# One layer of a hybrid decoder on one core: rings of their own for raw weights and norm scratch, a preloaded first output projection, a paired end of the input projection, and a later use of the mixers' room

## Chip, cores and metric

The kernel runs on one core of one Trainium2 chip. The metric is the device time of one execution in microseconds, median of three runs.

## What is computed

One layer (DEPTH is 1) of a decoder trunk, in fp32, on 2048 prompt tokens and on 8 further sequences of one token each (the samples):

```python
h = rmsnorm(x, norm_mix);  p = h @ w_in                     # 1024 -> 31 column tiles of 128, and 12 columns for b, a
y = concat(gdn(p_a), rwkv7(p_b), hgrn2(p_c))                # three mixers, chunked recurrences over 64 tokens
x = x + y @ w_out
h = rmsnorm(x, norm_ffn);  u = silu(h @ w_gate) * (h @ w_up)  # 2816 = 22 tiles of 128
x = x + u @ w_down
y = rmsnorm(x, norm_final)
```

The final states of the three mixers, for the prompt and for the samples, are outputs too.

## The kernel before, in words

Tokens lie on the free axis: four column blocks q = 0 to 3 of 512, 512, 512 and 520 tokens (the last holds the 8 samples and is worked in two halves of 260). Channels lie on the partitions. Every large product is a sum of eight k steps of three matmuls each (`mm3`, lines 369 to 376): operands are split into a high and a low part (ACT copies the high part, DVE subtracts), and high x high, high x low and low x high are added up in one PSUM bank. A product of 8 k steps is thus 24 matmuls of 512 columns.

**Two programs are woven into one.** `emit` (from line 1499) has a generator `gemm()` that yields one product after another: the input projection of q = 0, 1, 2, 3 (31 tiles each, `proj`), then for each q `out_proj(q)` and `ffn(q)`. The mixers (gdn g, rwkv r, hgrn h; 8 units for each q, named g00 = gdn, q 0, unit 0, and so on, last h31) are generators too, run by `Driver.turn`. After each round of mixer steps `turn` emits products until `made` has reached `due`, which grows by `RATES[q]` matmuls a round. `out_proj(q)` waits until all units of q are done. What is emitted so gets its place on the five queues (PE, DVE, ACT, POOL, SP) from a scheduler that works with times of its own. Each queue is worked in order: an instruction that waits, a DMA on SP too, holds up what stands behind it. Every tile pool is a ring: a tile may be written when the tile that had its place `bufs` requests earlier is no longer read. So a ring ties together whatever shares its tag, in the order of requests.

**Rings that the change touches.** Pool `x2` (8 tiles of 128x520) serves three users. `load_w` (line 312) takes two tiles of it for the raw halves of each weight tile of the input projection of q = 0 (line 324); a raw half is loaded (line 328), split by ACT (329) and DVE (330) into a tile of the ring `hl` (4 halves, so two weight tiles), and stored for the later q (337). `stats_x(q)` (for q over 0 called in the middle of the projection of q - 1, at unit number `AT` = 5) takes twelve through `S`: seven squares, the projection's b and a columns `pba`, and `be`, `ba` of the function `ba`. `out_proj` takes eight for the residual x2 (line 531). For q = 1 to 3 the weights come back split (line 344).

**The end of the mixers.** When all mixer units are done, `D.end()` returns and `K.late = 1` is set. From there weights are loaded into the mixers' scratch tiles instead of `hl` (the ring of lane A with 29 tiles, line 318; loads in line 342), four weight tiles ahead (`stream`, `AHEAD`), `bank` uses the mixers' PSUM banks as well, and the FFN's temporaries take lane P. The stores of the final states (`finals`, line 1429) are emitted there too.

**The turn of the blocks.** xs is a ring of 8 tiles, one per k: xs of the next block (`split_x`) or the mixers' output (`out_proj`, line 512: loaded by DMA in line 515 into the low half of an xs tile, then split in place) can be written when the last product that reads that k is past it.

```python
        while self.made < self.due and self.product():      # Driver.turn
            pass
    D.end()                                                  # emit, the end
    K.late, K.lane = 1, "A"
    K.finals()
    while D.product() is not None:
        pass
```

## Time and profile before

| | |
|---|---|
| median of 3 runs | 3219.25 us (3217.04 to 3220.66) |
| profiled execution: its time / its span | 3220.64 us / 3218.8 us |
| PE busy | 3079.2 us (96%), 24812 matmuls |
| DVE, ACT busy | 2194.7 us (68%), 1176.6 us (37%) |
| mean granted clock of PE | 0.973 |
| DMA | 628 MB, 195 GB/s over the span |

The profile page gives sums over the whole span and forty slices of it. Its views used below are tables of stretches (busy time of each engine, granted clock, DMA share), the waits (which engine waited for whom), the instructions in order of time of one engine or of SP's DMA queue (SPq), the groups of instructions by line, and the DMA issues. A granted clock of 1.00 is 2.4 GHz and 0.50 is 1.2 GHz; a mean between them tells what part of a stretch ran at either.

### The profile page before, as it was taken

What the parts mean: (1) busy time and instruction counts of PE and PEld (TensorE: products, weight loads), DVE (VectorE), ACT (ScalarE), POOL (GpSimd) and SP (SyncE); (2) the same over time, 40 slices, a digit from 0 to 9 for tenths busy, and PEclk for the clock granted to TensorE, in tenths of its full rate; (3) what the DMA queues carried; (4) which work ended last, traced back from release to release, by engine and by line L of the source; (5) the groups of instructions that cost most, each with busy time, mean ns of one, the idle gap of its engine ahead of it and who ended that gap; (6) DMA issues with size and microseconds to landing.
All of it is one profiled execution on the core that took longest, in us unless ns stands there. A gap on an engine that the chain in (4) does not pass through costs nothing.

```text
span 3218.8 us, 62719 instructions
## 1 busy us (share of the span) xinstructions
PE 3079.2 (96%) x24812; PEld 2464.1 (77%) x24812; DVE 2194.7 (68%) x5424; ACT 1176.6 (37%) x2051; POOL 12.1 (0%) x41
## 2 busy tenths in 40 slices
PE   8999999989998999999999999999999899999998
PEld 6667777768987677677766777777777678999998
DVE  6884667587678888886978788778767632443334
ACT  5443233244335444544454434253523220221002
POOL 0000000000000000000000000000000000000000
PEclk9989999999998999999999999999999899999999
DMA  9777666656655666677664455556544365755552
GB/s 316 257 245 250 188 188 212 195 158 190 190 179 171 223 231 202 225 239 255 231 215 140 149 171 155 173 183 197 179 152 166 107 215 188 248 174 184 188 185 91
DMA packets 393699, 628.00 MB, mean 195 GB/s; under 512 B 173181, under 2 KB 177533, under 8 KB 393405
## 3 DMA queue, kind: packets, MB, share of 16 engines
q1 hardware_dynamic: 392316, 622.93, 60.1%
q8 instruction: 195, 3.19, 0.4%
q10 hardware_dynamic: 1088, 1.07, 0.1%
q14 instruction: 100, 0.81, 0.1%
HBM read 456.77 MB, written 167.14 MB: 194 GB/s over the span
## 4 chain that ended last, share of the span: by engine, by line
PE 68%; DVE 14%; DMA 9%; ACT 4%; issue 2%; SPq 2%; DVEq 0%; ACTq 0%
PE psp L374 5%; PE psp L376 5%; PE psp L375 5%; PE pd L374 4%; PE pd L375 4%; PE pd L376 4%; PE pfg L374 4%; PE pfg L376 4%; PE pfu L375 4%; PE pfu L374 4%; PE pfu L376 4%; PE pfg L375 4%; DMA rw_wu<-wu 1%; PE pso L374 1%; PE pso L375 1%
## 5 line engine op out<-in xcount | busy, mean ns | idle before, releaser
L374 PE MATMUL psp<-xs,w_in 128*128 128x512 f32 (+1 forms) x1240 | 445.3, 360 | 20.1 <-ACT xs L406 8.4
L375 PE MATMUL psp<-xs,w_in 128*128 128x512 f32 (+1 forms) x1240 | 444.7, 359 | 0.8 <-DVE xs L407 0.8
L376 PE MATMUL psp<-xs,w_in 128*128 128x512 f32 (+1 forms) x1240 | 442.6, 358 | 2.0 <-DVE w_in L330 1.8
L374 PEld LDWEIGHTS psp<-xs,w_in 128*128 128x128 f32 x1240 | 236.1, 190 | 60.2 <-ACT xs L406 9.0
L376 PEld LDWEIGHTS psp<-xs,w_in 128*128 128x128 f32 x1240 | 235.5, 190 | 44.4 <-issue 5.5
L375 PEld LDWEIGHTS psp<-xs,w_in 128*128 128x128 f32 x1240 | 236.0, 190 | 37.3 <-issue 2.7
L592 DVE TENSOR_TENSOR x<-pd,x 128x512 f32<-128x512 f32 (+1 forms) x240 | 137.1, 581 | 105.3 <-PE pd L376 104.1
L374 PE MATMUL pfg<-xhs,w_wg 128*128 128x512 f32 x448 | 181.0, 404 | 4.3 <-ACT w_wg L329 3.4
L375 PE MATMUL pfg<-xhs,w_wg 128*128 128x512 f32 x448 | 180.6, 403 | 2.5 <-DVE xhs L550 2.5
L374 PE MATMUL pd<-u,w_wd 128*128 128x512 f32 x432 | 173.5, 409 | 9.1 <-ACT w_wd L329 3.2
L571 ACT ACTIVATE t<-t 128x512 f32<-128x512 f32 (+1 forms) x110 | 60.0, 546 | 333.1 <-DVE t L570 332.8
L376 PE MATMUL pfg<-xhs,w_wg 128*128 128x512 f32 x448 | 180.5, 403 | 0.3 <-DVE w_wg L330 0.3
L374 PE MATMUL pfu<-xhs,w_wu 128*128 128x512 f32 x448 | 180.1, 402 | 0.0
L375 PE MATMUL pfu<-xhs,w_wu 128*128 128x512 f32 x448 | 180.0, 402 | 0.0
L376 PE MATMUL pfu<-xhs,w_wu 128*128 128x512 f32 x448 | 179.6, 401 | 0.0
L375 PE MATMUL pd<-u,w_wd 128*128 128x512 f32 x432 | 173.7, 403 | 1.6 <-DVE u L360 1.6
L376 PE MATMUL pd<-u,w_wd 128*128 128x512 f32 x432 | 172.2, 400 | 1.5 <-DVE w_wd L330 1.4
L282 ACT ACT_TABLE_LOAD x91 | 116.8, 1283 | 104.0 <-PE oss_g L272 16.5
L359 ACT ACTIVATE u<-t 128x512 fp32r<-128x512 f32 (+1 forms) x110 | 60.0, 545 | 249.9 <-DVE t L574 249.8
L471 DVE TENSOR_TENSOR p<-psp,ri 128x512 f32<-128x512 f32 (+1 forms) x155 | 89.9, 581 | 71.1 <-PE psp L376 68.8
L375 PE MATMUL pd<-u,hw_wd 128*128 128x260 f32 (+1 forms) x448 | 137.6, 308 | 0.0
L376 PE MATMUL pd<-u,lw_wd 128*128 128x260 f32 (+1 forms) x448 | 137.1, 308 | 0.0
(642 smaller groups left out, 7383.5 us busy)
## 6 DMA issues: line engine op xcount, KB each, us to landing
w_in<-sw_in SPq DMA_DIRECT2D x186, 512.0 KB, 4.0
w_wg<-sw_wg SPq DMA_DIRECT2D x68, 512.0 KB, 3.4
w_wu<-sw_wu SPq DMA_DIRECT2D x68, 512.0 KB, 3.3
w_wd<-sw_wd SPq DMA_DIRECT2D x64, 512.0 KB, 4.1
sw_in<-w_in SPq DMA_DIRECT2D x62, 512.0 KB, 5.3
s_p<-p SPq DMA_DIRECT2D x93, 256.0 KB, 4.0
sw_wg<-w_wg SPq DMA_DIRECT2D x44, 512.0 KB, 3.4
sw_wu<-w_wu SPq DMA_DIRECT2D x44, 512.0 KB, 2.9
```

What stands on the lines that cost most here:

```text
L282: p = self.nc.scalar.preload_act_table_set("natural_log_exp_and_others")
L359: nc.scalar.activation(out[:, 0], src, AF.Copy)
L374: nc.tensor.matmul(ps, lhsT=hi[:, ws], rhs=xs[:, 0, xc], start=start, stop=False)
L375: nc.tensor.matmul(ps, lhsT=hi[:, ws], rhs=xs[:, 1, xc], start=False, stop=False)
L376: nc.tensor.matmul(ps, lhsT=lo[:, ws], rhs=xs[:, 0, xc], start=False, stop=stop)
L471: nc.vector.tensor_tensor(p[:, c0:c0 + cn], ps, rstd[q][:, c0:c0 + cn], ALU.mult)
L571: nc.scalar.activation(t, g, AF.Tanh, scale=0.5)
L592: nc.vector.tensor_tensor(x2[d][:, c0:c0 + cn], ps, x2[d][:, c0:c0 + cn], ALU.add)
```

## The change

`S` gets a ring of 5 tiles of its own and a new `R` one of 3; the raw halves take `R`, the statistics take `S`, and of the residual's tiles three take `R` and five `S`. The raw tiles of `out_proj(0)` are requested before the last unit's tiles of the projection of q = 3, from the pool `u` (`raw_pairs`), so that `out_proj(0)` only splits. For q under 3 the last two tiles of the projection (29 and 30) are computed in one pass over k (`gemm8x2`). At the end, the final states are stored and six more products are emitted before `late` is set.

```diff
--- before.py
+++ after.py
@@ -238,7 +238,10 @@
 
     def S(self, name):
 
-        return self.x2p.tile([128, QW], F32, tag="x2", name=name)
+        return self.x2p.tile([128, QW], F32, tag="x2b", name=name, bufs=5)
+
+    def R(self, name):
+        return self.x2p.tile([128, QW], F32, tag="x2a", name=name, bufs=3)
 
     def F(self, name, lane="C"):
 
@@ -321,7 +324,7 @@
             hi, lo = hi.bitcast(F32R), lo.bitcast(F32R)
             if q == 0:
                 if key[0] == "in":
-                    raw = self.S(f"r{name}")[:, 0:512]
+                    raw = self.R(f"r{name}")[:, 0:512]
                 else:
                     raw = self.wp.tile([128, 512], F32, tag="raw", name=f"r{name}", bufs=2)
                 with ExitStack() if key[0] == "in" else self.tc.issue_after(self.mark.ins):
@@ -375,6 +378,14 @@
         nc.tensor.matmul(ps, lhsT=hi[:, ws], rhs=xs[:, 1, xc], start=False, stop=False)
         nc.tensor.matmul(ps, lhsT=lo[:, ws], rhs=xs[:, 0, xc], start=False, stop=stop)
 
+    def gemm8x2(self, ws, xs, c0, n, names):
+
+        pss = [self.bank(name)[:, :n] for name in names]
+        for k in range(8):
+            for ps, w in zip(pss, ws):
+                self.mm3(ps, w, k, xs[k], c0, n, k == 0, k == 7)
+        return pss
+
     def gemm8(self, w, xs, c0, n, name):
 
         ps = self.bank(name)[:, :n]
@@ -504,15 +515,18 @@
             self.rsqs([(r[:, c0:c0 + cn], ps, None)], 1.0 / D, load=not more)
         return r
 
-    def out_proj(self, q):
+    def out_proj(self, q, raws=()):
 
         nc = self.nc
         t0, n = QS[q]
         xs = []
         for e in range(8):
             t = self.new_xs(f"mxs{q}_{e}")
-            raw = t[:, 1, :n].bitcast(F32)
-            nc.sync.dma_start(raw, self.s_mix[q][e])
+            if raws:
+                raw = raws[e][:, :n]
+            else:
+                raw = t[:, 1, :n].bitcast(F32)
+                nc.sync.dma_start(raw, self.s_mix[q][e])
             self.split(t[:, :, :n], raw)
             xs.append(t)
         x2, acc, wait, res = [], None, [], []
@@ -528,7 +542,7 @@
             self.finish()
             for i, (c0, cn), ps in wait:
                 if c0 == 0:
-                    x = self.x2p.tile([128, QW], F32, tag="x2", name=f"x2_{q}_{i}")
+                    x = (self.R if i < 3 else self.S)(f"x2_{q}_{i}")
                     x2.append(x)
                 cs = slice(c0, c0 + cn)
                 nc.vector.tensor_tensor(x[:, cs], ps, res[i][:, cs], ALU.add)
@@ -1436,6 +1450,7 @@
 AT = 5
 STEP = 2
 AHEAD = 4
+SLACK = 6
 RATES = (12.25, 14.25, 15.25, 19.25)
 ROOM = (1, 1, 2, 1)
 
@@ -1524,6 +1539,9 @@
                         load[q + 1] = K.load_x(q + 1)
                 if i == AT and q < 3:
                     rstd[q + 1] = K.stats_x(q + 1, load[q + 1])
+                if q == 3 and i == len(order) - 1:
+                    assert not D.left[0]
+                    mixed = K.raw_pairs(K.s_mix[0], "mix")
                 for m in ms:
                     if w:
 
@@ -1533,6 +1551,12 @@
                         K.load_consts()
                         K.proj((q,), m, xs, rstd, None, lambda: K.stats_x(0, load[0]), held)
                         held, w = [second], None
+                    elif q < 3 and ms is order[-1][0] and m in ms[-2:]:
+                        if not held:
+                            ws = [K.load_w(K.io["w1"][j], ("in", j), q) for j in ms[-2:]]
+                            held = K.gemm8x2(ws, xs[q], 0, G, [f"psp{q}_{j}" for j in ms[-2:]])
+                        K.proj((q,), m, xs, rstd, None, None, held[:1])
+                        held = held[1:]
                     else:
                         K.proj((q,), m, xs, rstd, None, None, held)
                         held = []
@@ -1545,7 +1569,7 @@
             while D.left[q]:
                 K.finish()
                 yield 0
-            yield from K.out_proj(q)
+            yield from K.out_proj(q, mixed if q == 0 else ())
             yield from K.ffn(q)
         K.finish()
 
@@ -1566,8 +1590,10 @@
             if q == 2:
                 D.side(samples.pop(0), 3)
     D.end()
+    K.finals()
+    for _ in range(SLACK):
+        D.product()
     K.late, K.lane = 1, "A"
-    K.finals()
     while D.product() is not None:
         pass
```

The operations and their numbers are the same on PE, DVE and POOL (19008 matmul and transpose operations, 5426 on DVE); ACT has 13 more table loads by the placing of functions (182 before, 195 now), and SP issues 12 DMAs fewer, since 12 weight halves come as one DMA and not two. What moves is order.

**SP, the input projection of q = 0, around weight tiles 11 and 20** (rw_in: a raw half; sw_in: a store of a split half; s_nr, inF, inU: the inverse of a mixer unit; s_be: a result of stats_x(1)). Before:

```order
L328 DMA rw_in_11_0_2016<-w1 128x512
...
L478 DMA s_p0_147<-p0_11_2022 128x512
L652 DMA s_nr00_179<-N_r00_1299 32x8x32 x4
L663 DMA inF0_204<-s_nr00_179 16x8x16 x2
L660 DMA inU_r00_1367<-s_nr00_179 32x16x16 x2
...
L486 DMA p_g01_1872<-s_p0_147 128x512
...
L486 DMA pkr01_2600<-s_p0_147 128x512
L758 DMA s_be1_143<-be1_2143 6x512
L328 DMA rw_in_20_0_2163<-w1 128x512
```

and now:

```order
L331 DMA rw_in_11_0_2016<-w1 128x512
L340 DMA sw_in_10_0_1_1936<-w_in_10_0_1931 128x1024
L331 DMA rw_in_20_0_2163<-w1 128x512
L666 DMA s_nr00_179<-N_r00_1299 32x8x32 x4
L340 DMA sw_in_11_0_0_2013<-w_in_11_0_2008 128x1024
L677 DMA inF0_204<-s_nr00_179 16x8x16
L674 DMA inU_r00_1367<-s_nr00_179 32x16x16 x2
L677 DMA inF0_204<-s_nr00_179 16x8x16 x3
...
L340 DMA sw_in_11_0_1_2020<-w_in_11_0_2015 128x1024
L331 DMA rw_in_20_0_2170<-w1 128x512
L331 DMA rw_in_21_0_2248<-w1 128x512
```

The raw halves of tile 20 stood 33 places behind the last of tile 11 and behind s_nr, p_g, pkr and s_be; now the first of them stands two places behind and ahead of s_nr, and the second behind s_nr and the loads that hang on it.

**SP, the beginning of out_proj(0)** (mxs0: the mixers' output; cbuf, pbuf: inputs of the samples; rw_o: raw weights of w_out). Before:

```order
L515 DMA mxs0_0_12489<-s_mix0_151 128x512
L515 DMA mxs0_1_12493<-s_mix0_151 128x512
...
L478 DMA s_p3_150<-p3_30_12397 128x520
L1416 DMA cbuf_12482<-cbuf 128x27x8
L1417 DMA pbuf_12483<-pbuf 128x11x8
L1418 DMA o_cs<-cbuf 16x1152
...
L515 DMA mxs0_4_12505<-s_mix0_151 128x512
...
L328 DMA rw_o_0_0_12522<-wo 128x512
```

and now:

```order
L489 DMA s_p3_150<-p3_30_12409 128x520
L1430 DMA cbuf_12494<-cbuf 128x27x8
L1431 DMA pbuf_12495<-pbuf 128x11x8
L1432 DMA o_cs<-cbuf 16x1152
L331 DMA rw_o_0_0_12526<-wo 128x512
L1434 DMA o_tail<-tail_116 128x93
...
L331 DMA rw_o_0_0_12533<-wo 128x512
L340 DMA sw_o_0_0_0_12530<-w_o_0_0_12525 128x1024
```

The eight loads of the mixers' output are gone from here (they stand on the places 575 to 611 of the queue now, where it had the places 732 to 745), and rw_o follows o_cs.

**PE, the last mixer unit h31** (pfu2, pfg2, pd2: gate, up and down products of ffn(2); be, bd, pl, ptk: steps of h31; px: a step of r32). Before:

```order
L376 MATMUL pfu2_11_28295<-xhs2_7_26027,w_wu_11_2_28267 128x512
...
L271 MATMUL be_h31_27481<-hi_be_h31_27482,blkr_92 128x256
...
L271 MATMUL bd_h31_27489<-hi_bd_h31_27490,blkr_92 128x512
...
L1223 MATMUL pl0_h31_27586<-lv_h31_27507 64x64 x2
...
L1223 MATMUL pl0_h31_27624<-lv_h31_27611 64x64 x8
...
L1105 MATMUL px_r32_27617<-Z0_r32_25720,W00_r32_25774 64x64
...
L725 MATMUL ptk_h31_27999<-cst_88,kx_h31_27958 128x128 x4
...
L374 MATMUL pfg2_12_28427<-xhs2_0_26006,hw_wg_12_2_28378 128x512
```

and now:

```order
L275 MATMUL be_h31_27485<-lo_be_h31_27487,blkr_92 128x256
...
L377 MATMUL pfu2_12_28416<-xhs2_6_26028,w_wu_12_2_28388 128x512
...
L378 MATMUL pfu2_12_28416<-xhs2_6_26028,w_wu_12_2_28388 128x512
...
L1237 MATMUL pl0_h31_27590<-lv_h31_27511 64x64 x2
...
L378 MATMUL pfu2_13_28485<-xhs2_4_26022,w_wu_13_2_28457 128x512
...
L377 MATMUL pd2_0_28524<-u2_10_28102,w_wd_3_0_2_28520 128x512
...
L1237 MATMUL pl0_h31_27628<-lv_h31_27615 64x64 x2
...
L379 MATMUL pd2_0_28524<-u2_12_28390,w_wd_3_0_2_28520 128x512
...
L1237 MATMUL pl0_h31_27732<-lv_h31_27721 64x64 x2
...
L377 MATMUL pd2_3_28570<-u2_10_28102,w_wd_3_1_2_28554 128x512
...
L739 MATMUL ptk_h31_28003<-cst_88,kx_h31_27962 128x128 x4
```

Before, no product stands between the last matmul of pfu2_11 and the first of pfg2_12. Now the steps of h31 stand between products of tiles 12 and 13 and of the down projection behind them. Counted over all rows, 8394 product matmuls stood ahead of the last step of h31 (po_h31) and 8609 do now; ahead of the last step of g32 it was 8280 and is 8303; ahead of that of g00, early in the program, 930 and 978.

## Rows read from the trace of the kernel before

**Rows 1.** The profile page, span, busy time and the forty slices of the granted clock and of the DMA engines.

```profile
span 3218.8 us, 62719 instructions
PE 3079.2 (96%) x24812; PEld 2464.1 (77%) x24812; DVE 2194.7 (68%) x5424; ACT 1176.6 (37%) x2051; POOL 12.1 (0%) x41
PEclk9989999999998999999999999999999899999999
DMA  9777666656655666677664455556544365755552
```

**Rows 2.** The table of stretches: microseconds from:to and their length, then for each engine its busy time (x instructions), the granted clock of TensorE, the busy share of the DMA engines, GB/s.

```profile
20.00:140.00 120.00, 115.24 (x515) 87.72 (x516) 94.58 (x183) 60.92 (x98) 0.79 (x8) 0.99 0.93 320
145.00:185.00 40.00, 30.27 (x354) 19.40 (x342) 36.74 (x101) 21.56 (x37) 0.20 (x2) 0.62 0.35 98
185.00:235.00 50.00, 50.00 (x359) 38.46 (x358) 38.72 (x96) 19.73 (x36) 0.20 (x2) 1.00 0.86 291
1010.00:1040.00 30.00, 18.47 (x268) 13.55 (x267) 23.79 (x73) 20.12 (x35) 0.00 (x0) 0.63 0.68 186
2535.00:2570.00 35.00, 19.55 (x291) 15.64 (x291) 32.74 (x96) 11.70 (x20) 0.53 (x1) 0.62 0.19 62
2570.00:2640.00 70.00, 62.62 (x351) 48.24 (x351) 28.03 (x53) 20.02 (x26) 0.00 (x0) 0.87 0.61 194
2640.00:2700.00 60.00, 60.00 (x260) 48.54 (x259) 17.80 (x26) 5.06 (x8) 0.00 (x0) 1.00 0.64 220
2616.00:2640.00 24.00, 23.63 (x91) 19.09 (x92) 12.41 (x20) 5.30 (x8) 0.00 (x0) 0.88 0.37 118
```

**Rows 3.** SP's DMA queue in order of time, 118 to 184 us: start, length of the issue, line, tile.

```profile
120.49 0.33 SPq L328 DMA_DIRECT2D rw_in<-w  x1
...
144.92 0.43 SPq L478 DMA_DIRECT2D s_p<-p  x1
...
152.64 1.80 SPq L652 DMA_DIRECT2D s_nr<-N_r  x4
...
164.79 0.34 SPq L486 DMA_DIRECT2D p_g<-s_p  x1
...
170.09 0.30 SPq L758 DMA_DIRECT2D s_be<-be  x1
...
170.44 7.72 SPq L328 DMA_DIRECT2D rw_in<-w  x5
```

**Rows 4.** The waits of SP's queue from 140 to 200 us: line, whom it waited for, us in total, times, longest.

```profile
SPq L652 <- DVE N_r L1058: 7.2, 1, 7.2
SPq L486 <- DVE kq_g L815: 7.1, 1, 7.1
SPq L758 <- DVE be L757: 1.8, 1, 1.8
```

**Rows 5.** SP's DMA queue in order of time, 1012 to 1038 us.

```profile
1013.63 1.80 SPq L515 DMA_DIRECT2D mxs<-s_mix  x4
...
1016.60 4.68 SPq L1417 DMA_DIRECT2D pbuf<-pbuf  x1
...
1023.21 1.83 SPq L515 DMA_DIRECT2D mxs<-s_mix  x4
1025.09 0.97 SPq L328 DMA_DIRECT2D rw_o<-wo  x2
```

**Rows 6.** The waits of TensorE from 1010 to 1040 us.

```profile
PE pso L374 <- ACT w_o L329: 5.7, 1, 5.7
```

**Rows 7.** TensorE in order of time, 2534 to 2570 us; in brackets the idle time before a row and what ended it.

```profile
2534.42 0.50 PE L376 MATMUL pfu<-xhs,w_wu 128*128 128x512 f32 x1
...
2548.61 1.13 PE L1223 MATMUL pl_h<-lv_h 64*64 64x64 f32 x32 [2.59 <-DVE lv_h L1215]
...
2554.27 1.61 PE L1223 MATMUL pl_h<-lv_h 64*64 64x64 f32 x32 [3.61 <-DVE att_h L1226]
...
2569.57 0.80 PE L374 MATMUL pfg<-xhs,hw_wg 128*128 128x512 f32 x1
```

**Rows 8.** The waits of SP's queue from 2535 to 2616 us.

```profile
SPq L342 <- PE po_h L1270: 6.2, 2, 3.3
SPq L342 <- DVE kx_h L1239: 3.5, 1, 3.5
```

**Rows 9.** TensorE in order of time at two turns of the block, q 0 to 1 and q 2 to 3.

```profile
255.88 0.47 PE L374 MATMUL psp<-xs,w_in 128*128 128x512 f32 x1 [1.37 <-DMA w_in<-sw_in]
...
776.11 0.58 PE L374 MATMUL psp<-xs,w_in 128*128 128x260 f32 x1 [2.91 <-DMA w_in<-sw_in]
```

**Rows 10.** Groups of instructions by line: line, engine, operation, tiles, shape, count | busy us, mean ns of one | idle time of the engine before them and what ended most of it.

```profile
L282 ACT ACT_TABLE_LOAD x91 | 116.8, 1283 | 104.0 <-PE oss_g L272 16.5 <-PE pnf L501 15.0 <-PE yv_r L272 11.9
L592 DVE TENSOR_TENSOR x<-pd,x 128x512 f32<-128x512 f32 (+1 forms) x240 | 137.1, 581 | 105.3 <-PE pd L376 104.1
L330 DVE TENSOR_TENSOR w_in<-rw_in,w_in 128x512 fp32r<-128x512 f32 x62 | 42.0, 682 | 13.2 <-ACT w_in L329 12.7
L329 ACT ACTIVATE w_in<-rw_in 128x512 fp32r<-128x512 f32 x62 | 38.3, 627 | 60.2 <-PE psp L376 24.8 <-DMA sw_in<-w_in 18.1 <-DMA s_p<-p 8.6
```

**Rows 11.** DMA issues from 20 to 140 us: tile, queue, count, KB each, median us to landing.

```profile
sw_in<-w_in SPq DMA_DIRECT2D x36, 512.0 KB, 5.4
rw_in<-w SPq DMA_DIRECT2D x32, 256.0 KB, 5.4
```

## The prediction

> **What bounds the kernel now.** The first look goes to the page's busy times: TensorE is busy for 3079.2 of 3218.8 us and no other engine for more than 68% [rows 1]. So time can come only from two things: TensorE standing still, which is 3218.8 - 3079.2 = 139.6 us in all, and TensorE running at the lower of its two levels. The profile puts the mean granted clock at 0.973, which is 0.027 x 3218.8 = 87 us given away. The sum is some 227 us, and the slices of the clock show that much of it lies in a few places [rows 1]. The second look goes to the table of stretches there [rows 2]; the loss of a stretch is its length less TensorE's busy time, and its length times one less the clock:
>
> - 145 to 185 us: 40 - 30.27 = 9.7 us idle, 40 x 0.38 = 15.2 us of clock, **24.9 us**.
> - 1010 to 1040: 11.5 and 11.1, **22.6 us**.
> - 2535 to 2640: 15.5 + 7.4 idle, 13.3 + 9.1 of clock, **45.3 us**.
>
> These 175 us hold 93 of the 227 us. The third look is at what TensorE had there: SP's queue, the waits and the instructions in order of time.
>
> **Part 1, rings of their own for raw weights and norm scratch: 15 us gained.** SP issues the last raw half of weight tile 11 at 120.49 us and the first of tile 20 at 170.44 [rows 3]. Between them SP waits 7.2 us for DVE's N_r, 7.1 for kq_g and 1.8 for `be` [rows 4]: the raw tiles had asked for their places behind the scratch of `stats_x(1)`, and were put behind the work that it goes with. From the end of tile 11 TensorE has only mixer steps, each waiting for DVE. In the change the first raw half of tile 20 stands ahead of s_nr, and its split stands among the mixers' DVE work. TensorE then has products in the hole. It can't all be won. DVE is busy for 36.74 of these 40 us, and each product brings it two splits and one scaling, 2 x 0.68 + 0.58 = 1.9 us [rows 2, 10]; five products bring 9.7 us, where 3.3 are free, so mixer steps move behind, into 185 to 235, where DVE has 11.3 us left and TensorE none [rows 2]. The order says how far that goes: at the last step of g00 the program is 48 product matmuls further on, and at 60 us for 260 matmuls one takes 0.231 us [rows 2], so 11.1 us. Bounds: 25 (the whole loss) and 5 (DVE gives back most). I take 15, nearer to the order's 11 than to 25. The same change takes raw tiles from 8 to 3; while the first loads run, the DMA engines are busy for 0.93 of 20 to 140 us and TensorE for 115.24 of 120 [rows 2], so that stretch I leave at no change; what happens if 3 are too few is a rival below.
>
> **Part 2, the mixers' output loaded early: 6 us gained.** At 1013.63 SP issues four loads of it, as soon as xs tiles come free; then come the sample inputs, one of which takes 4.68 us to issue, then four more loads at 1023.21, and only then the raw weights of w_out at 1025.09 [rows 5]. The first product of `out_proj(0)` waits 5.7 us for their split [rows 6]. The change takes eight loads out, 1.80 + 1.83 = 3.6 us of issue [rows 5]; the slow sample load stays ahead of the weights. So weights and first product come 3.6 us earlier, and as the stretch that follows runs at a mean clock of 0.63, a shorter stop gives back about 2.4 us more. Bounds: 14 (the weights, too, land faster with eight loads fewer before them) and 0 (the first product waits for the eight splits on ACT instead). The new loads stand far ahead, where SP has waits already; I cost them at nothing, and at one block's weight load late, 2.9 us, if that cover goes [rows 9].
>
> **Part 3, six products before the mixers' room is used: 34 us gained.** After the last matmul of pfu2_11 at 2534.42 no product runs until pfg2_12 at 2569.57 [rows 7]: its weights (hw_wg) are bound for scratch of h31 and h30, and their loads wait for kx_h and po_h to be done [rows 8]. TensorE does h31's small steps, each after DVE (2.59 and 3.61 us for two of them) [rows 7], at a clock of 0.62 [rows 2]. Now pfg2_12 to pd2_3 come from the ordinary ring and stand between the steps. From the last step of g32 to that of h31 the order has 306 product matmuls (8609 - 8303) where it had 114: 192 x 0.231 = 44 us of work, about the 45.3 us lost. What of the loss stays: DVE was busy for 32.74 of 35 us [rows 2] and gets five operations for each of two tiles and four evictions more, 14 x 0.58 = 8 us [rows 10], and behind the mixers the down projection still waits for the last u; I leave 11 us. 45 - 11 = 34. Bounds: 42 (all but 3) and 17 (the clock stays down, below).
>
> One rule speaks against this part. What stands there now is mixer steps of 64 columns mixed with single product matmuls that go round over several PSUM banks. The kernel before has such a round over banks from 2616 to 2640, where products of pd2_0 to pd2_7 take turns by single matmuls; TensorE was busy there for 23.63 of 24 us and was granted 0.88 [rows 2]; so the clock comes back in it, late. The Trainium skill, TensorE: Matmul & The Clock Gate, section "A second HAM failure mode: psum-queue depth-cycling", says that cycling through PSUM banks leaves small gaps in which the clock keeps falling and rising, so that throughput suffers even with TensorE hardly idle. By the row the clock loss of 22.4 us goes nearly all; by the page it would stay, and this part would be 17 and not 34. I go by the row.
>
> **Part 4, the paired last tiles: 0.** The turns of the block cost 1.37 and 2.91 us of idle time, both ended by a load of weights [rows 9], not by xs. The pair lets go of xs tiles in a slower rhythm, which helps the splits; but it holds all four halves of the weight ring to its end, so that the next block's second half can be loaded only then. Bounds: +4 and -4.
>
> **Part 5, 13 more table loads: -2.** 13 x 1.28 = 16.7 us on ACT [rows 10], which is busy for 37% [rows 1]. Bounds: 0 and -17; nearly all lie beside other work, so -2.
>
> **Sum.** 15 + 6 + 34 + 0 - 2 = 53. The profiled execution took 3220.6 us, so 3167.6; it stands 1.4 us above the median of the runs, 3219.25, and against that the forecast is **3166 us**. All the rest is reshuffled too, some of it better and some worse; I see no sign in it.
>
> **The rivals.**
>
> - **The front doesn't pay.** DVE (92% busy in 145 to 185) and the DMA engines (0.93 in 20 to 140) take parts 1 and 2 back. For it: the mixers' steps there wait for DVE anyway. Against: DVE and DMA both have room right after. 3219 - 34 + 2 = 3187.
> - **The clock stays down in the last part** (the page's rule, as a mechanism here: short steps and single matmuls over changing banks). 3219 - (53 - 17) = 3183. Against it is the 0.88 of 2616 to 2640 [rows 2].
> - **Three raw tiles starve the first projection: slower.** A half is consumed in 12 x 0.231 = 2.8 us, three in 8.3. A place comes back after landing, 5.4 us [rows 11], and the split, 0.63 + 0.68 [rows 10], so 6.7: 1.6 us to spare, while SP has waits of 7 us [rows 4]. If the cycle is 11.1 us on average, 62 halves cost (11.1 - 8.3) / 3 = 0.93 us each, 58 us, and part 1 is gone: 3219 - 38 + 58 = 3239. It decides from a cycle of some 10.5 us on, where 45 us eat up the rest and the bound of a measurement. Against: before ACT's splits the idle time is ended by matmuls (24.8 us) and by stores of the ring hl (18.1), not by raw loads [rows 10]; hl, two weight tiles ahead, is the cushion. The Trainium skill, DMA: Bandwidth & Descriptors, section "Anatomy of one DMA", has a fixed 2.0 us and 436 GB/s, fitted on another issuing path; an estimate from it for 256 KB is 2.6 us, and with it this rival would have hardly a chance. The trace's 5.4 us decides, with the DMA engines at 0.93.
> - **Nothing moves.** The scheduler's order gives back elsewhere what it wins here: DVE is the bound of the mixers' stretches in the middle, and holes open there. 3219. The order has the products 23 to 215 matmuls ahead at the three mixer units that are counted, which speaks against it.
>
> **How the numbers follow.** Forecast 0.74; clock down 0.10; front doesn't pay 0.06; nothing moves 0.05; slower 0.05. The range: with all upper bounds 25 + 14 + 42 + 4 = 85, 3134; with the lower bounds of the first three, 5 + 0 + 17, less 2, 3199, which takes in two of the rivals. A measurement of this kernel tells 0.2% or 6.4 us from no change; faster by more than that: 0.74 + 0.10 + 0.06 = 0.90, within 0.05, slower 0.05.
>
> **What would show it.** Right: raw loads of SP go on between 120 and 170 us, and the clock of that stretch is near 1.00; w_out's raw weights are issued within 8 us of the last projection; around the last mixer unit TensorE is busy for over 90% at a clock over 0.9; idle time and clock loss together fall from 227 to some 175 us. Wrong: TensorE waiting for ACT or DVE at w_in in the first 250 us with raw loads behind them (three tiles too few); a clock of 0.6 to 0.8 at the last unit although TensorE is busy; or idle time and clock loss unchanged from 2535 us on, which would say that the mixers and not the products set the end of that stretch.

## The result and the profile after

The changed kernel takes **3189.18 us**, median of four runs (3185.85 to 3195.49); the kernel before took 3218.14 beside it (3213.22 to 3220.66). The ratio is 0.9914, 95% interval 0.9894 to 0.9934: 29 us faster, where 53 were forecast. The profiled execution took 3185.85 us with a span of 3184.1, so between the two traces lie 34.7 us of span, and these are what has to be explained.

The page after, with the same lines as [rows 1] (span; busy us, share and count of each engine; the forty slices of the granted clock and of the DMA engines):

```profile
span 3184.1 us, 62691 instructions
PE 3063.0 (96%) x24812; PEld 2442.2 (77%) x24812; DVE 2189.0 (69%) x5424; ACT 1196.6 (38%) x2064; POOL 12.3 (0%) x41
PEclk9999999999999999999999999999999999999999
DMA  8877666657656766677764454557554465755552
```

No slice of the clock is down to 8 any more. The table of stretches after, as [rows 2], with one more of 50 to 110 us (length, then busy us of PE, PEld, DVE, ACT, POOL, granted clock, DMA share, GB/s):

```profile
20.00:140.00 120.00, 110.42 (x530) 83.07 (x533) 90.21 (x175) 56.42 (x92) 1.02 (x8) 0.94 0.90 293
50.00:110.00 60.00, 50.42 (x218) 37.65 (x216) 43.17 (x80) 28.31 (x47) 0.50 (x5) 0.91 0.89 281
145.00:185.00 40.00, 38.37 (x293) 27.82 (x294) 33.83 (x84) 21.06 (x37) 0.20 (x2) 1.00 0.84 262
185.00:235.00 50.00, 45.95 (x235) 33.24 (x234) 43.33 (x116) 24.18 (x38) 0.20 (x2) 0.95 0.70 219
1010.00:1040.00 30.00, 22.02 (x117) 15.24 (x116) 22.66 (x84) 15.20 (x29) 0.00 (x0) 0.77 0.62 164
2535.00:2570.00 35.00, 33.42 (x338) 25.29 (x340) 31.01 (x84) 9.88 (x14) 0.41 (x1) 1.00 0.34 115
2570.00:2640.00 70.00, 66.50 (x424) 52.12 (x417) 24.61 (x54) 18.05 (x24) 0.00 (x0) 1.00 0.79 261
2640.00:2700.00 60.00, 56.10 (x231) 45.19 (x231) 24.74 (x38) 8.64 (x13) 0.00 (x0) 0.94 0.51 167
```

The hole at 145 to 185 us is filled (38.37 of 40 us at clock 1.00, where it was 30.27 at 0.62), and so is that around the last mixer unit (33.42 of 35 at 1.00, where it was 19.55 at 0.62). But new holes stand on both sides of the first: 50 to 110 us has 9.6 us of idle time and a clock of 0.91, and 185 to 235, full before, has 4.1 us idle at 0.95.

**An account that adds up.** Below, the loss of a stretch is its idle time and, of its busy time alone, the part that the clock took: busy x (1 - clock), summed over slices of 10 us. (The prediction took its clock loss from the whole length, so that idle time at the lower clock counted twice: its 227 us are 199.6 so.) What is left of the span is busy time at full clock, here called work. Every row of this table is worked out from one profiled execution; "between" counts, in the order of instructions, the product matmuls that stand between the last step of mixer unit g32 and that of h31. The ratios are against the kernel before as it ran beside each kernel: 3216 us beside e1 to e4, 3217 beside e5 to e8, 3218 beside the change and e9 to e11, and 3212 beside e12.

| kernel | median us | ratio to before (95%) | span | loss 0-140 | 140-250 | 1010-1060 | 2480-2700 | all | work | between |
|---|---|---|---|---|---|---|---|---|---|---|
| before | 3218 | 1 | 3218.8 | 17.0 | 21.0 | 18.6 | 37.0 | 199.6 | 3019.2 | 114 |
| the change | 3189 | 0.9914 (0.9894-0.9934) | 3184.1 | 27.9 | 10.5 | 12.4 | 11.1 | 154.3 | 3029.8 | 306 |
| e1 rings | 3218 | 1.0007 (0.9996-1.0019) | 3210.7 | 27.6 | 10.0 | 17.7 | 33.5 | 195.0 | 3015.7 | 152 |
| e2 early load | 3193 | 0.9926 (0.9910-0.9943) | 3192.9 | 19.2 | 21.5 | 8.2 | 35.8 | 180.0 | 3012.9 | 114 |
| e3 six products | 3196 | 0.9933 (0.9914-0.9951) | 3195.4 | 19.0 | 20.8 | 20.1 | 9.3 | 176.7 | 3018.7 | 312 |
| e4 pair | 3186 | 0.9904 (0.9887-0.9920) | 3183.6 | 17.5 | 20.5 | 13.3 | 11.1 | 162.1 | 3021.5 | 315 |
| e5 change, five raw places | 3180 | 0.9882 (0.9868-0.9896) | 3175.7 | 16.4 | 7.1 | 7.2 | 0.9 | 148.5 | 3027.2 | 349 |
| e6 change, no rings | **3160** | 0.9825 (0.9812-0.9838) | 3158.0 | 14.8 | 20.1 | 5.9 | 0.0 | 140.6 | 3017.4 | 350 |
| e7 pair and early load | 3171 | 0.9855 (0.9841-0.9869) | 3169.1 | 18.1 | 21.4 | 6.9 | 9.8 | 153.1 | 3016.0 | 315 |
| e8 change, no six products | 3213 | 0.9988 (0.9978-0.9998) | 3211.5 | 27.5 | 10.8 | 11.8 | 36.5 | 186.3 | 3025.2 | 114 |
| e9 change, no pair | 3187 | 0.9902 (0.9885-0.9919) | 3194.0 | 28.8 | 10.7 | 14.0 | 8.3 | 165.3 | 3028.7 | 303 |
| e10 change, first rate 13.25 | 3173 | 0.9859 (0.9838-0.9879) | 3169.2 | 25.2 | 11.4 | 7.4 | 3.0 | 150.4 | 3018.8 | 343 |
| e11 e6, first rate 13.25 | 3169 | 0.9846 (0.9826-0.9866) | 3161.7 | 18.0 | 20.3 | 7.2 | 3.2 | 147.4 | 3014.3 | 343 |
| e12 e5, first rate 14.25 | 3170 | 0.9866 (0.9849-0.9883) | 3164.4 | 15.1 | 3.1 | 7.0 | 0.0 | 136.6 | 3027.8 | 444 |

A profiled execution can stand 6 to 9 us to either side of its kernel's median (e1, e9), so differences of a few us in one column of one row are not read.

For the change the account of the 34.7 us is: loss 45.3 less, of which 0 to 250 us brings -0.4 (10.5 won, 10.9 lost), 1010 to 1060 6.2, 2480 to 2700 25.9, the long middle from 1060 to 2480 14.3, the rest -0.9 by the same slices; and 10.6 us more of work.

### The profile page after: what moved, and what is told of

The parts are those of the page before. It is cut to its first block, busy times and chain, and to the rows that moved or that the text cites. A ratio compares the mean times of both kernels' runs of the same rounds, so it can differ in the third digit from the quotient of the medians.

```text
span 3184.1 us, 62691 instructions
## 1 busy us (share of the span) xinstructions
PE 3063.0 (96%) x24812; PEld 2442.2 (77%) x24812; DVE 2189.0 (69%) x5424; ACT 1196.6 (38%) x2064; POOL 12.3 (0%) x41
## 4 chain that ended last, share of the span: by engine, by line
PE 68%; DVE 13%; DMA 11%; ACT 4%; SPq 2%; issue 2%; DVEq 0%; ACTq 0%
PE psp L377 5%; PE psp L379 5%; PE psp L378 5%; PE pfg L378 4%; PE pfg L377 4%; PE pfg L379 4%; PE pfu L377 4%; PE pfu L378 4%; PE pfu L379 4%; PE pd L377 4%; PE pd L379 4%; PE pd L378 4%; PE pso L377 1%; PE pso L378 1%; PE pso L379 1%
## 5 line engine op out<-in xcount | busy, mean ns | idle before, releaser
L377 PE MATMUL pfg<-xhs,w_wg 128*128 128x512 f32 x464 | 188.2, 406 | 7.3 <-ACT w_wg L332 4.8
L378 PE MATMUL pfg<-xhs,w_wg 128*128 128x512 f32 x464 | 188.8, 407 | 3.1 <-DVE xhs L564 3.1
L377 PE MATMUL pd<-u,w_wd 128*128 128x512 f32 x448 | 179.3, 409 | 10.4 <-DVE x L606 7.0
L379 PE MATMUL pfg<-xhs,w_wg 128*128 128x512 f32 x464 | 187.1, 403 | 0.1
L377 PE MATMUL pfu<-xhs,w_wu 128*128 128x512 f32 x464 | 186.5, 402 | 0.0
L378 PE MATMUL pfu<-xhs,w_wu 128*128 128x512 f32 x464 | 186.3, 402 | 0.0
L379 PE MATMUL pfu<-xhs,w_wu 128*128 128x512 f32 x464 | 185.0, 399 | 0.0
L378 PE MATMUL pd<-u,w_wd 128*128 128x512 f32 x448 | 178.9, 400 | 0.6 <-DVE u L363 0.6
L379 PE MATMUL pd<-u,w_wd 128*128 128x512 f32 x448 | 178.9, 400 | 0.0
L377 PE MATMUL pd<-u,hw_wd 128*128 128x260 f32 (+1 forms) x432 | 128.2, 307 | 3.9 <-ACT u L362 3.9
L378 PE MATMUL pd<-u,hw_wd 128*128 128x260 f32 (+1 forms) x432 | 131.3, 305 | 0.0
```

Of the source, the lines that this page charges most:

```text
L377: nc.tensor.matmul(ps, lhsT=hi[:, ws], rhs=xs[:, 0, xc], start=start, stop=False)
L378: nc.tensor.matmul(ps, lhsT=hi[:, ws], rhs=xs[:, 1, xc], start=False, stop=False)
L379: nc.tensor.matmul(ps, lhsT=lo[:, ws], rhs=xs[:, 0, xc], start=False, stop=stop)
```

## The experiments

**The four parts one by one, each alone on the kernel before.** e1 takes the rings:

```diff
     def S(self, name):
-        return self.x2p.tile([128, QW], F32, tag="x2", name=name)
+        return self.x2p.tile([128, QW], F32, tag="x2b", name=name, bufs=5)
+    def R(self, name):
+        return self.x2p.tile([128, QW], F32, tag="x2a", name=name, bufs=3)
...
-                    raw = self.S(f"r{name}")[:, 0:512]
+                    raw = self.R(f"r{name}")[:, 0:512]
...
-                    x = self.x2p.tile([128, QW], F32, tag="x2", name=f"x2_{q}_{i}")
+                    x = (self.R if i < 3 else self.S)(f"x2_{q}_{i}")
```

e2 the early load:

```diff
+                if q == 3 and i == len(order) - 1:
+                    assert not D.left[0]
+                    mixed = K.raw_pairs(K.s_mix[0], "mix")
...
-            yield from K.out_proj(q)
+            yield from K.out_proj(q, mixed if q == 0 else ())
```

e3 the six products:

```diff
     D.end()
+    K.finals()
+    for _ in range(SLACK):
+        D.product()
     K.late, K.lane = 1, "A"
-    K.finals()
```

e4 the pair:

```diff
+                    elif q < 3 and ms is order[-1][0] and m in ms[-2:]:
+                        if not held:
+                            ws = [K.load_w(K.io["w1"][j], ("in", j), q) for j in ms[-2:]]
+                            held = K.gemm8x2(ws, xs[q], 0, G, [f"psp{q}_{j}" for j in ms[-2:]])
+                        K.proj((q,), m, xs, rstd, None, None, held[:1])
+                        held = held[1:]
```

Expected of e1:

> The kernel before with the rings alone (R of 3, S of 5). Theory A (read from the trace after): the hole at 145 to 185 us is filled (12 to 25 us won there), but raw loads come late at 50 to 110 us (13 us lost), and DVE gives back the rest: between 3214 and 3224, that is no more than 4 us from 3218. Theory B (the prediction's part 1): 15 us won, 3203. Theory C (three raw tiles starve the projection by more than the hole is worth): 3230 or more. In the trace, by A, 145 to 185 us has TensorE busy over 37 of 40 us and 50 to 110 us under 53 of 60, with ACT waiting for raw loads.

of e2:

> The kernel before with the early load of the mixers' output alone. Theory A (milestones of the trace after: the first product of out_proj(0) 12 us earlier in relation to the projection's end): 3206. Theory B (the prediction's part 2): 3212. Theory C (those 12 us are reshuffled mixers and not the loads): 3218. By A the clock of 1010 to 1040 us is over 0.85 where it was 0.63; by C it stays under 0.75.

of e3:

> The kernel before with the six products (and the states' stores) ahead of the later use of the mixers' room alone. Theory A (milestones from the last step of g32 on): 17 to 18 us won, 3200, with the stretch from 2530 us filled at a clock near 1.00 and some 15 us lost again behind it by a longer tail of mixers. Theory B (the prediction's part 3): 34 us, 3184. Theory C (the clock stays down there): 17 us too, but with a granted clock of 0.6 to 0.8 from 2535 to 2600.

of e4:

> The kernel before with the paired last tiles of the projection alone. The prediction's part 4 and theory A: 0, between 3214 and 3222. Rival: the pair holds all four halves of the weight ring, the next block's first products wait for a load at each of three turns, 2 to 3 us each, 3225. Other rival: the rhythm in which xs tiles come free helps the splits, and the three turns give 2 to 3 us each, 3211.

Measured: +2, -24, -20 and -31 us against the kernel before beside them. The rings are worth nothing, as theory A had it; theory A is near for the six products too (3200 expected, 3196). For the early load all three theories were short: 3193, and the clock of 1010 to 1040 us came to 0.80, between their marks. Each of the three is worth most of what all four together bring; 75 us in sum, where the change has 29. The pair, which every theory had near nothing, is worth most. Its gain doesn't lie at the turns of the blocks but mostly at the far end: the loss of 2480 to 2700 us falls by 25.9 us, and by the six products alone by 27.7. So these two fill the same hole. The row of this place in the table of stretches shows it, for six kernels.

The kernel before:

```profile
2480.00:2700.00 220.00, 197.16 (x1376) 154.12 (x1376) 110.28 (x257) 48.04 (x72) 0.53 (x1) 0.90 0.49 164
```

The change:

```profile
2480.00:2700.00 220.00, 211.01 (x1379) 163.60 (x1378) 113.43 (x258) 51.47 (x75) 0.53 (x1) 0.98 0.56 186
```

E1, the rings:

```profile
2480.00:2700.00 220.00, 199.99 (x1194) 155.92 (x1193) 104.32 (x238) 45.41 (x66) 0.53 (x1) 0.91 0.51 172
```

E4, the pair:

```profile
2480.00:2700.00 220.00, 213.40 (x1229) 167.59 (x1229) 97.42 (x202) 40.78 (x57) 0.53 (x1) 0.97 0.58 194
```

E8 (below), the change without the six products:

```profile
2480.00:2700.00 220.00, 197.87 (x1331) 154.31 (x1324) 109.50 (x254) 48.80 (x72) 0.53 (x1) 0.90 0.50 169
```

E6 (below), the change without the rings:

```profile
2480.00:2700.00 220.00, 220.00 (x1237) 174.67 (x1236) 99.18 (x190) 44.45 (x64) 0.00 (x0) 1.00 0.63 211
```

The first number in front of a bracket is the one to read, TensorE's busy time of 220 us: 197 to 200 with the hole open, 211 to 213 where it is mostly filled, 220 where it is gone. How the pair does it is in the order: with it alone, 8079 product matmuls stand ahead of the last step of g32, where the kernel before has 8280. The mixers are 201 matmuls farther on against the products, a **lead** that leaves 315 to stand between the steps of the last three units, where there were 114.

**The change with one thing taken out.** In the order of instructions the whole change has 8303 ahead of g32: the pair's lead is gone in the company of the rings. Without the rings it is back, at 8079. e6 undoes e1's edit in the change, e8 undoes e3's, e7 joins e2's and e4's on the kernel before. e5 keeps the change and gives raw halves five places, three of R and two of a ring that stands empty at that time:

```diff
-                    raw = self.R(f"r{name}")[:, 0:512]
+                    self.nraw = getattr(self, "nraw", 0) + 1
+                    if self.nraw % 5 < 3:
+                        raw = self.R(f"r{name}")[:, 0:512]
+                    else:
+                        raw = self.wp.tile([128, 512], F32, tag="raw", name=f"r{name}", bufs=2)
```

Expected of e6:

> The change without its rings: early load, pair and later use of the mixers' room together. Theory A (the rings let products into the front that delay the mixers by 12 to 18 us from g00 to h01, and this lead is missing at the program's end; without them the pair's 31 us stay, the early load adds its 12 us at the beginning of out_proj(0), and the six products add up to 13 us of what is still lost from 2570 to 2590): 3162 to 3173, and in the trace g32 ends some 60 us earlier than in the kernel before. Theory B (whatever is filled in one place opens in another; all versions end between 3185 and 3192): 3187. Theory C (the prediction's sum without its part 1): 3178.

of e5:

> The whole change, but raw halves of the first projection take five places in turn and not three (three of R, two of the ring that the raw halves of the later weights have). Theory A (three places are too few and cost the 13 us lost from 50 to 110 us): 3176, with ACT waiting for raw loads under 8 us in 40 to 110 where the whole change has 22. Theory B (the front's gain is given back whatever the number of places, because TensorE's mixer steps wait for DVE, 185 to 235 us): 3188, and what is won at 50 to 110 is lost again by the end of the first projection. In the order of instructions 1079 product matmuls stand ahead of the last step of g00, where the whole change has 978.

of e7:

> The kernel before with the pair and the early load of the mixers' output, without rings and without the six products. Theory A: 3173 (31 us of the pair, 12 of the early load; the 10 us at the turn from q 2 to 3 are won by either and count once). Against e6_norings it tells what the six products are worth where the pair has filled the hole: by A 0 to 10 us. Theory B (versions end between 3185 and 3192 whatever is joined): 3187.

of e8:

> The whole change without the six products ahead of the later use of the mixers' room. Theory A (with the rings the mixers have lost the lead that the pair alone gives them; in the order of instructions 8280 product matmuls stand ahead of the last step of g32 and 8394 ahead of that of h31, as in the kernel before, so the hole around the last unit is open again): 3203 to 3207, with TensorE busy under 85 of the 105 us around the last unit. Theory B (the pair fills that hole in any company, and the six products are idle talk beside it): 3189.

Measured: e6 3160, e5 3180, e7 3171, e8 3213. All four are nearest to theory A, whose figures are off by 2 us (e6, e7), 4 (e5) and 6 (e8). Without the rings the change is 29 us faster and beats both kernels. With the rings and without the six products nearly nothing of pair and early load is left (4 us; e8 against e7: 42 us, of which 26.7 are loss from 2480 to 2700 us and 9.2 work). e5 settles the cause of the loss in the front. In the waits of ACT from 40 to 110 us the change has (line, whom it waited for, us, times, longest):

```profile
ACT w_in L332 <- DMA rw_in<-w: 22.0, 7, 8.1
```

and e5:

```profile
ACT w_in L336 <- DMA sw_in<-w_in: 9.5, 8, 2.6
ACT w_in L336 <- DMA rw_in<-w: 2.4, 1, 2.4
```

With two more places the loss of 0 to 140 us falls from 27.9 to 16.4, about that of the kernel before (17.0). In all fourteen kernels it is 25 to 29 us with three places and 15 to 19 with five or eight. How three become too few shows SP's queue of the change, 42 to 74 us:

```profile
42.51 0.43 SPq L331 DMA_DIRECT2D rw_in<-w  x1
...
46.18 6.21 SPq L405 DMA_DIRECT2D raw_x<-xT  x8
...
56.35 2.86 SPq L331 DMA_DIRECT2D rw_in<-w  x3
...
72.68 0.43 SPq L331 DMA_DIRECT2D rw_in<-w  x1
```

Twice no raw half goes out for over 13 us, from the end of the issue at 42.51 until 56.35 and from the end of that at 56.35 until 72.68. In the second pause the scheduler put the next one behind sixteen loads and stores of the mixers and the projection. The pauses alone are not the harm, for the kernel before has them too, of 11 and 12 us:

```profile
44.57 0.50 SPq L328 DMA_DIRECT2D rw_in<-w  x1
...
56.26 3.06 SPq L328 DMA_DIRECT2D rw_in<-w  x3
...
59.84 0.43 SPq L328 DMA_DIRECT2D rw_in<-w  x1
...
72.50 1.29 SPq L328 DMA_DIRECT2D rw_in<-w  x2
```

What differs is the stock. At 56 us the kernel before had issued 19 raw halves and begun to split 15, the change 14 and 14; at 72.4 us it was 23 and 19 against 17 and 17. A half lasts 2.8 us by the prediction's count, so a pause of 13 us takes nearly five; eight places hold them and three do not. In the change ACT then stands still until the half issued at 72.68 has landed:

```profile
77.54 0.63 ACT L332 ACTIVATE w_in<-rw_in 128x512 fp32r<-128x512 f32 x1 [8.08 <-DMA rw_in<-w]
```

In e5, 40 to 72 us, one more goes out in between and the next is 1.7 us earlier; at 72.4 us it had issued 21 and begun to split 19:

```profile
56.37 2.36 SPq L335 DMA_DIRECT2D rw_in<-w  x3
60.19 0.33 SPq L335 DMA_DIRECT2D rw_in<-w  x1
...
70.94 0.45 SPq L335 DMA_DIRECT2D rw_in<-w  x1
```

e5's front is 19 us ahead at the end of the first projection (last product of q 0), yet 8 of these are gone by the end of q 1 and 11 by that of q 2, and the total gains 9 to 10. That total is not the front's gain kept, as theory A had it. By the slices e5 loses 14.9 us less than the change up to 250 us and 10.2 less from 2480 to 2700, but 9.5 more from 250 to 1010 and 15.3 more from 1060 to 2480. So theory A's figure for the total came near by luck; its cause for the front is what e5 shows.

**Is it the rings, or the weave that follows on them?** e9 leaves the pair out of the change. e10 and e11 put the change and e6 at another first rate; in the order both then have the same counts from unit g22 to the end.

```diff
-RATES = (12.25, 14.25, 15.25, 19.25)
+RATES = (13.25, 14.25, 15.25, 19.25)
```

Expected of e9:

> The whole change without the pair. Theory A (what the pair is worth is the mixers' lead that it gives, and with the rings that lead is gone; in the order of instructions 8290 product matmuls stand ahead of the last step of g32 and 8593 ahead of that of h31, where the whole change has 8303 and 8609): 3183 to 3193, no difference from the whole change's 3189. Theory B (the pair is worth its 31 us in any company): 3215 or more.

of e10:

> The whole change, with the first of the four rates of products per mixer round at 13.25 for 12.25. In the order of instructions 989 product matmuls stand ahead of the last step of g00, 6251 ahead of that of g22, 8194 of g32, 8537 of h31. Theory A (the rings are worth nothing in the front and cost only by the weave that follows on them; with this rate the weave from g22 on is the one that the kernel without rings has at the same rate): within 6 us of the next run, both 3163 to 3178. Theory B (the rings cost by themselves, from 40 to 760 us): 15 to 29 us above the next run. Theory C (the rate does nothing, since it only says in which order the work is put to the scheduler): 3189.

of e11:

> The change without its rings, with the first rate at 13.25 for 12.25. In the order of instructions 930 product matmuls stand ahead of the last step of g00, 6251 ahead of that of g22, 8194 of g32, 8537 of h31: the same from g22 on as in the run before. Theory A (the mixers' lead at g32 decides, 8194 where the change without rings has 8079 and the whole change 8303): 3163 to 3178. Theory B (the lead is of no weight, the absence of the rings is): 3160. Theory C (what is won without the rings hangs on one lucky weave): 3185 or more.

Measured: e9 3187, e10 3173, e11 3169. All as theory A had it. In the company of the rings and the six products the pair is worth nothing that these runs can tell (e9 has 303 matmuls between, the change 306). And where the weave from g22 on is alike, rings or none make 4 us, with intervals that overlap, not 29: e10 loses 25.2 us from 0 to 140 and 11.4 from 140 to 250, e11 18.0 and 20.3, in sum 36.6 and 38.3. So by themselves the rings cost little: 4 us here, and by the two intervals together hardly over 14. Most of the 29 us that they cost in the change comes of the weave that follows on them.

**Five places and a rate that gives a lead, together** (e5's edit, and 14.25 for 12.25):

> The whole change with five places for raw halves and the first rate at 14.25. In the order of instructions 6123 product matmuls stand ahead of the last step of g22, 8130 of g32, 8574 of h31, where the change without rings has 6225, 8079 and 8429. Theory A (the mixers' lead decides, and the front's gain of some 20 us that five places gave at 250 us is kept where the lead is not spent): 3150 to 3162, faster than any version so far or level with the fastest (3160). Theory B (the front's gain is spent by the later weave again, as with five places at the old rate): 3172 to 3182. Theory C (rings in any company keep the end of the program 25 us later): 3185.

Measured: 3170, between theories A and B. The kernel before ran at 3212 beside it, so by the ratio it stands at 3175 on the scale of the others, within theory B's range; theory A missed. The losses are the lowest of all kernels, 136.6 us, with 3.1 left from 140 to 250 and none at the end. But the stretch from 250 to 1010, which has no column in the table, loses 38.2 us, where e6 loses 23.1 (e5: 34.3, the change: 24.8). These 15 us are nearly all of the 16.7 by which e12 is ahead of e6 in the losses up to 250. And its work is 3027.8, 10 more than e6's. That eats the rest.

## Why the prediction came out as it did

The direction and the range were right; the sum of 53 was too large by 18 us against the profile (24 against the medians). Of its parts, 15 + 6 + 34, the runs show 0, 6 and 26, so 32 us. That the profiles differ by 34.7, so near to these 32, is luck: 14.3 us won in the middle, which nothing forecast, and 10.6 us of added work nearly cancel. The steps fared as follows.

- **Part 1 (15 us): wrong, 0.** The signs given as right came: raw loads go on through the hole at 145 to 185 us and the clock is 1.00. The sign given as wrong came as well: in the first 250 us TensorE waits 9.7 us for ACT's splits (4.9 before), and behind them ACT waits 22.0 us for raw loads from 40 to 110.

```profile
PE psp L377 <- ACT w_in L332: 9.7, 4, 3.2
```

  The step that failed is "that stretch I leave at no change": eight places to three moved the hole forward. The rival of three starving tiles had the mechanism, not the size: 50 to 110 us loses 13.6 us where it lost 1.7, and 0 to 140 10.9 more, not 58. What sets it is not the steady cycle of 6.7 us but the pauses of 13 us in SP's order, which a stock of three can't cover. The ring hl was no cushion for them: at 60.7 us TensorE had used all 14 halves that were split (168 product matmuls, 12 for each). e1 has the same front and gains nothing; e5 shows the number of places as the cause: with five, 0 to 250 us loses 23.5 us where the kernel before loses 38.0, and these 14.5 are about the 15 that the part was to bring.
- **Part 2 (6 us): right in its place, 6.2 us** from 1010 to 1060; from 1010 to 1040 the idle time is down by 3.6 us and the clock's loss by 1.8, where 3.6 and 2.4 were forecast. The weights' first issue is at 1017.84, 7.2 us after the end of the last projection (1010.64) and so within the 8 that were named; before it was 11.05. The stop for w_out's split is down from 5.7 to 2.7 us:

```profile
1014.23 2.82 SPq L1431 DMA_DIRECT2D pbuf<-pbuf  x1
...
1017.84 0.57 SPq L331 DMA_DIRECT2D rw_o<-wo  x1
```
```profile
PE pso L377 <- ACT w_o L332: 2.7, 1, 2.7
```

  Alone it is worth 10.4 us there and 24 in all; the other 14 are spread over the weave.
- **Part 3 (34 us): mechanism right, size 25.9.** What was mis-sized is the 45.3 that it was taken from: counted once, the stretch had lost 37.0. The 11 us to be left over came as 11.1, but that the figures meet is luck. Of the 11.1, the wait that was named, the down projection for the last u, is 3.9, one for h31's norm 2.1, short waits of the last steps 3.0, and the clock behind them 2.1; the 8 us of DVE's operations that were part of the forecast hardly show:

```profile
2634.27 0.50 PE L377 MATMUL pfu<-xhs,hw_wu 128*128 128x512 f32 x1 [2.06 <-ACT osq_h L296]
...
2644.00 1.22 PE L377 MATMUL pd<-u,hw_wd 128*128 128x512 f32 x2 [3.90 <-ACT u L362]
```

  Taken out of the change (e8) it costs 24 us.
- **The rule on PSUM cycling: not borne out.** The stretch of short steps between products over changing banks runs at a granted clock of 1.00, that is 2.4 GHz, for 105 us (2535 to 2640), with TensorE busy for 99.92 of them. The Trainium skill, TensorE: Matmul & The Clock Gate, section "A second HAM failure mode: psum-queue depth-cycling", tells of another kernel, in bf16, in which the clock kept falling and rising; here the trace doesn't agree with it, and going by the row was right. How near that kernel's pattern comes to this one no run here shows: in this stretch most products run in rows of some 8 to 29 matmuls of one tile between the steps.
- **Part 4 (0): right in the change, wrong by itself.** The pair doesn't work through the turns' idle time. What it moves lies some 1700 us behind the last of them, in the order of the last units. e9 bears out the 0, by a cause that I had not seen: the rings had undone it, as e8 shows, where pair and rings together leave the hole open.
- **Part 5 (-2): not told apart.** ACT's busy time rose by 20.0 us, of which 13 table loads are 16.7, on an engine busy for 38%.
- **"All the rest is reshuffled too ... I see no sign in it": here the sum failed most.** The middle from 1060 to 2480 us gave 14.3 us that nothing forecast; work took 10.6. By the spacing of starts on TensorE, idle time taken out and at full clock, the borders between products and other steps hold 305 us before and 330 after (657 and 703 changes from a product to a step), the other steps among themselves 437 and 428, the products among themselves 2274 and 2269. So the work that was added lies at the borders; there are more of them, and one costs the same (0.46 to 0.47 us for the two borders of a change, in all fourteen kernels). But the count alone doesn't tell the work: e10 has 695 changes, nearly as many, at 328 us, and yet the work of the kernel before, since its other steps take 421 us and its products 2266. Why these come cheaper in one weave than in another is open, and so is why the rings with one rate make 3029.8 of the work and with another 3018.8.
- **The signs and the rivals.** By the prediction's own count the loss fell from 227 to 169 us (121.1 idle, 47.8 of clock), further than the 175 named, while the span fell by only 34.7: of these 58 us, 13 are idle time counted twice and 10.6 went into work. "The front doesn't pay" stands nearest with 3187, but not by its mechanism: part 2 did pay, and part 1 fell to the number of places. That rival has something of e5 and e12, where what five places win in the front is largely lost again up to 1010 us. "The clock stays down" (3183) is out by the clock of 1.00, and "nothing moves" by the interval.

The loss at the program's end goes with the last column of the table, whichever edit made the count (six products, pair, rate, or five places): with 114 to 152 product matmuls between the last three units' steps the loss from 2480 to 2700 us is 33 to 37 us, with 303 to 315 it is 8 to 11, and with 343 and more 0 to 3, in all fourteen kernels. Of the 26.1 us of span between the change and e6, this place holds 11.1 and work 12.4. Not settled is why the scheduler gives the mixers this lead with the pair and takes it back with the rings; e10 shows that a small change of a rate moves it as well.

## What to carry to other kernels

Where two programs are woven by a scheduler, a part's worth hangs on the weave that comes out: three parts worth 20 to 31 us each made 29 together with a fourth that is worth nothing alone, and leaving this fourth out made 57 of it. Before a forecast, count in the order of instructions, for each part alone and for the whole without it, how much work of the bounding engine is left beside each known hole: here that count went with the loss of the hole in all fourteen kernels. Size a ring of loads by the longest pause of the queue that issues them, not by the steady cycle: here pauses of 13 us against 2.8 us a load. Sum losses so that idle time and clock are each counted once.

## What the runs showed of the hardware

The DMA issue of one sample input (`pbuf`, 128 x 11 x 8) took 4.68 us before and 2.82 now, behind four loads fewer. It took 3.3 to 5.5 us in the four kernels that issue two to five loads of the mixers' output shortly ahead of it, and 2.6 to 3.0 in the ten that load it early. Twelve executions of e1 lie between 3212.1 and 3229.8 us, so a difference of 0.2% is told only by several runs of each.
